# A list scheduler's price table and the place of one group of sums in a two-block kernel on one core

## Chip, cores and metric

The kernel runs on one core of one Trainium2 chip. The metric is the device time of one execution in microseconds (us), the median of several runs. In the profile PE is TensorE (matmuls), PEld its weight loads, DVE is VectorE, ACT is ScalarE, POOL is GpSimd and SP issues DMAs.

## The reference, cut to what matters

Two blocks of two layers each run one after the other on 512 tokens of width 1024 in fp32. The second block, around which the change lies, also carries 256 context tokens:

```
def hybrid_layer(l, x, xc, ...):                      # twice, l = 0 and 1
    h  = rms_norm(x,  norm_g) * (1 + scale)   + shift      # 512 tokens
    hc = rms_norm(xc, norm_g) * (1 + scale_c) + shift_c    # 256 tokens
    aq, ak, av, az, bq, ..., cq, ck, cv, cz, gm = split(h @ w_in)
    y_a = differential attention,  4 heads
    y_b = bidirectional mLSTM,     4 heads
    y_c = neighbourhood attention, 8 heads, done two at a time
    g   = sigmoid(gm)                                      # 3 x 1024 columns
    x   = x + gate * (sum_n g_n * (y_n @ w_br[n])) @ w_out
```

Before it, the first block has a recurrent mixer, a convolutional feed-forward layer, a forgetting attention with a spatial gate, and a second feed-forward layer. The reference computes in fp32 throughout.

## The kernel before

**Precision.** A weight matmul is done as three fp32r matmuls: each operand x is split into hi (an ACT copy to fp32r) and lo (a DVE subtraction x - hi), and `mm3` adds hi*hi, hi*lo and lo*hi in PSUM. `K.H` and `K.L` hold the hi and lo halves of the normed activations, eight tiles of 128 rows by 768 columns (512 tokens, then 256 of context). `modulated` writes them at the start of each layer of the second block: per row tile one DVE multiplication, one ACT copy to H and one DVE subtraction to L.

**The gate product.** The projection `gm` (3072 output columns) is done by a Strassen-Winograd scheme with 7 products in place of 8. It needs sums of quarters of the operand, made once per layer by `halves(n)`, a generator of four steps. One step takes two row tiles: two POOL additions H + L into tiles x and y, four DVE additions or subtractions of halves of x and y, and two splits (ACT copy, DVE subtraction) into four tiles that stay alive until the last gate product. In layer 0 (n = 384) all 768 columns take part, in layer 1 (n = 256) 512 columns. `gm_pair` makes two of 24 output tiles: it loads two weight tiles, makes their sums on POOL, and runs the seven products.

**Order of work.** `Block2.run` makes for each layer a list of 12 heads: 4 of branch C (two attention heads each), 4 of A, 4 of B. A head has a `prep` generator (projections of q, k, v; the splits and copies that stack them for PE, in `Kern.stack`) and an `attend` or `scan` generator (scores, softmax, products). At index i the loop weaves the second generator of head i with the `prep` of head i + 1, with `GM[i]` gate pairs (none before i = 3), and, in the kernel before, with `halves` at i = 0.

**The scheduler.** Nothing is issued in that order at once. `Order` records every instruction with its reads, writes and an estimated duration (`_cost`); `flush` then runs a list schedule. It keeps one clock for each engine; on each engine it scans up to 30 instructions whose producers have been placed, in the order of recording, takes the first that can start on time or else the one that starts first, and places the earliest of all engines. It adds a lag after each producer (190 to 250 ns between engines). The estimates thus set the fixed order of each engine's queue; they set no waits. The scheduler knows nothing of engines that slow one another.

**Slots.** All working tiles of the second block come from 36 slots called "s". An instruction may take a new tile only when at most `WINDOW` = 30 tiles of this kind recorded before it are still waiting for a slot, and only when its own tiles and up to 8 earlier ones would find free slots.

All instructions are recorded through a helper, so most rows of the profile carry its line, L486.

Of the kernel before, what the change touches and what calls it, by code (L numbers as in the profile page):

```python
# [199 lines left out]
class Order:  # L200
# [133 lines left out]
    @staticmethod  # L334
    def _cost(eng, op, a, k, aps, psum):
        size = 1
        n_in = 0
        for key, x in aps:
            n = 1
            for _, c in list(x.ap)[1:]:  # L340
                n *= c
            size = max(size, n)
            if key not in ("out", "accum_out", 0, "bias") and n > 4:
                n_in += 1
        if op == "dma_start":
            x = k["out"]
            b = 4
            for _, c in x.ap:
                b *= c
            return ("dma", b / 300.0)  # L350
        if eng == "pe":
            x = k["out"] if "out" in k else a[0]
            n = 1
            for _, c in list(x.ap)[1:]:
                n *= c
            if op == "transpose":
                return max(n, 64) / 1.2 + 3
            if k["rhs"].dtype == F32R:
                return n / 2.4 * (1 if n >= 256 else 2) + 3
            return max(n, 128) / 0.6 * (1 if x.ap[0][1] > 64 else 0.62) + 4  # L360
        if eng == "act":
            return (52 if psum else 94) + size * 0.833 + (93 if k.get("accum_out") is not None else 0)
        if eng == "pool":
            return 146 + (2.1 if op == "tensor_tensor" else 3.3) * size
        if op == "reciprocal":
            return 70 + 6.5 * size
        two = not psum and n_in <= 1 and op in ("tensor_copy", "tensor_scalar", "memset")
        return 95 + size / (1.92 if two else 0.96)


    def flush(self, keep=()):
# [120 lines left out]
def weave(*gens):  # L492

    live = [[0.5 / n, 1.0 / n, g] for n, g in gens]
    while live:
        x = min(live, key=lambda x: x[0])
        x[0] += x[1]
        if next(x[2], live) is live:
            live.remove(x)


def chain(*gens):

    def run():
        for _, g in gens:
            yield from g
    return sum(n for n, _ in gens), run()
# [656 lines left out]
FIRST = 7  # L1164

GM = (0, 0, 0, 1, 1, 1, 1, 2, 2, 2, 1, 1)


class Block2:
# [742 lines left out]
    def run(self, out, dbg, es):  # L1912
        K, nc = self.K, self.nc
        self.pool = es.enter_context(self.tc.tile_pool(name="slots", bufs=1))
        lat, ctx = K.part(0, T), K.part(T, TC)
        for l in range(2):
            self.l = l
            full = l == 0
            ya, yb, yc = [], [], []
            if l == 1:  # L1920
                for u in EARLY:
                    self.early[(1, *u)] = self.unit(*u, lat, ctx)
            hb, first = self.branch_b(lat, ctx, full, yb)
            heads = self.branch_c(lat, ctx, full, yc) + self.branch_a(lat, ctx, full, ya) + hb
            mg = []
            self.yd = {b: K.dr.tile([128, 4, 768], F32, name=f"yd{l}{b}") for b in (0, 2)}
            self.gd = [K.dr.tile([128, 8, 768], F32, name=f"gd{l}{b}") for b in range(3)]
            gm = [self.gm_pair(b, m) for b in (2, 0, 1) for m in range(0, 8, 2)]
            n = 384 if full else 256
            weave(heads[0][0])  # L1930
            for i in range(12):
                g = [gm.pop(0) for _ in range(GM[i])]
                weave(heads[i][1], *([heads[i + 1][0]] if i < 11 else []), *([first] if i == FIRST else []),
                      *([(4, self.halves(n))] if i == 0 else []),
                      *([chain(*((8, x) for x in g))] if g else []))
            for b, y in ((2, yc), (0, ya), (1, yb)):
                self.merge(b, y, mg, full, b == 1)
            X, S = self.out_proj(full, None if full or dbg == 6 else out)
            if dbg == 5 + l:
                for m in range(8):  # L1940
                    nc.sync.dma_start(out=out[:, m], in_=X[m])
                return
            if full:
                R, _ = S[0].rstd()
                for m in range(8):
                    nc.sync.dma_start(out=self.xd[:, m], in_=X[m])
                self.norm_lat(1, X, R, self.s)
# [36 lines left out]
```

## Time and profile before

| | us |
|---|---|
| median of 3 runs | 2893.25 |
| lowest, highest | 2891.59, 2897.68 |
| profiled execution, own time | 2893.14 |
| its span, first to last instruction | 2891.3 |
| PE busy (modelled) | 2832.5 |
| DVE, ACT, POOL busy | 2057.0, 1308.7, 402.3 |
| mean granted TensorE clock | 0.993 of full |

The span leaves 1.8 us of the execution's own time outside. Matmuls overlap in the pipeline and their ends are modelled, so PE's busy time is an upper bound of its work.

### The profile page before, as it was taken

The numbers are of one execution on the slowest core, as the hardware profiler recorded it, in microseconds if no ns is written. First come the engines' busy times: TensorE is split into PE (matmuls) and PEld (weight loads), VectorE is DVE, ScalarE is ACT, GpSimd is POOL, SyncE is SP. The second block draws the span as 40 slices with busy tenths as digits, with TensorE's granted clock in tenths as the row PEclk, the third lists the DMA queues.
The fourth block names the chain that finished last, engine by engine and source line by source line (L and its number), as shares of the span: only waits on it lengthen the run. The fifth ranks groups of instructions, "written<-read, shape, count | busy, mean of one in ns | idle before, by whom it ended". The sixth has DMA issues, their size and how long they took to land. (4 is left out here: it accounts for less than half of the span.)

```text
span 2891.3 us, 42552 instructions
## 1 busy us (share of the span) xinstructions
PE 2832.5 (98%) x16266; PEld 2444.7 (85%) x16266; DVE 2057.0 (71%) x4038; ACT 1308.7 (45%) x2469; POOL 402.3 (14%) x296
## 2 busy tenths in 40 slices
PE   8999999999999999999999999999999999999998
PEld 6888888887888888789999989998878889989887
DVE  7778678468786875865677686575686677787765
ACT  6344234455442343664455453341346554554433
POOL 1010000010100002200211132120220122232202
PEclk9999999999999999999999999999999999999999
DMA  4333433322333423211122132155322122233362
GB/s 157 125 119 123 136 139 111 105 96 96 124 111 129 144 87 124 79 61 63 56 77 75 55 108 92 68 162 173 124 74 93 63 76 75 78 100 103 103 211 95
DMA packets 113243, 302.63 MB, mean 105 GB/s; under 512 B 11656, under 2 KB 25352, under 8 KB 113040
## 3 DMA queue, kind: packets, MB, share of 16 engines
q1 hardware_dynamic: 112896, 299.91, 30.6%
q8 instruction: 128, 2.10, 0.3%
q14 instruction: 75, 0.61, 0.1%
q10 hardware_dynamic: 144, 0.00, 0.0%
HBM read 272.26 MB, written 27.61 MB: 104 GB/s over the span
## 5 line engine op out<-in xcount | busy, mean ns | idle before, releaser
L486 PE MATMUL P<-H,wl 128*128 128x512 f32 (+2 forms) x2648 | 962.2, 364 | 8.2 <-DVE wl L486 8.2
L486 PE MATMUL P<-H,wh 128*128 128x512 f32 (+2 forms) x2648 | 963.9, 365 | 2.7 <-ACT H L486 2.6
L486 PE MATMUL P<-L,wh 128*128 128x512 f32 (+2 forms) x2648 | 962.4, 364 | 3.4 <-DVE L L486 3.4
L486 ACT ACTIVATE wh<-ws 128x1024 fp32r<-128x1024 f32 (+3 forms) x450 | 436.4, 972 | 765.0 <-PE P L486 660.3
L486 DVE TENSOR_TENSOR wl<-ws,wh 128x1024 fp32r<-128x1024 f32 (+3 forms) x450 | 522.1, 1162 | 208.2 <-ACT wh L486 203.1
L486 PEld LDWEIGHTS P<-H,wl 128*128 128x128 f32 x2648 | 500.7, 189 | 88.0 <-DVE wl L486 10.5
L486 PEld LDWEIGHTS P<-L,wh 128*128 128x128 f32 x2648 | 500.5, 189 | 85.3 <-DVE L L486 6.5
L486 PEld LDWEIGHTS P<-H,wh 128*128 128x128 f32 x2648 | 500.6, 189 | 83.8 <-ACT H L486 3.7
L486 PE MATMUL P<-s,wh 128*128 128x256 f32 (+2 forms) x1344 | 329.7, 333 | 0.0
L486 PE MATMUL P<-t,wh 128*128 128x512 f32 x960 | 302.1, 395 | 0.7 <-ACT t L486 0.7
L486 ACT ACTIVATE s<-P 128x512 f32<-128x512 f32 (+3 forms) x436 | 189.9, 471 | 225.4 <-PE P L486 202.2
L486 PE MATMUL P<-s,s 128*128 128x128 f32 (+4 forms) x1616 | 246.6, 292 | 12.8 <-DVE s L486 12.7
L486 PEld LDWEIGHTS P<-s,wh 128*128 128x128 f32 x1344 | 228.9, 188 | 17.3
L486 PEld LDWEIGHTS P<-s,s 128*128 128x128 f32 (+1 forms) x1616 | 215.3, 190 | 32.8 <-issue 9.7
L486 PE MATMUL P<-s,wl 128*128 128x256 f32 (+2 forms) x672 | 222.3, 331 | 2.2 <-DVE wl L486 2.2
L486 PEld LDWEIGHTS P<-t,wh 128*128 128x128 f32 x960 | 179.9, 188 | 44.3 <-ACT t L486 0.9
L486 ACT ACTIVATE s<-s 128x768 f32<-128x768 f32 (+7 forms) x226 | 153.0, 694 | 110.2 <-DVE s L486 94.3
L486 POOL TENSOR_TENSOR s<-s,s 128x512 f32<-128x512 f32 (+2 forms) x87 | 112.4, 1299 | 583.3 <-DVE s L486 307.3
L486 DVE TENSOR_TENSOR s<-s,s 128x512 f32<-128x512 f32 (+8 forms) x205 | 179.3, 881 | 19.6 <-DMA s<-cmd 10.5
L486 PE MATMUL P<-t,wl 128*128 128x512 f32 x480 | 189.6, 395 | 0.0
L486 ACT ACTIVATE s<-P,tn 128x512 f32<-128x512 f32 (+1 forms) x226 | 119.0, 535 | 106.2 <-DVE tn L486 104.7
L486 ACT ACTIVATE t<-t 128x512 f32<-128x512 f32 (+4 forms) x162 | 97.8, 611 | 125.1 <-DVE t L486 124.2
(149 smaller groups left out, 3571.7 us busy)
## 6 DMA issues: line engine op xcount, KB each, us to landing
ws<-in_w2in SPq DMA_DIRECT2D x136, 512.0 KB, 3.3
ws<-in_up SPq DMA_DIRECT2D x88, 512.0 KB, 3.2
wm<-in_w_mod SPq DMA_DIRECT2D x48, 512.0 KB, 4.4
ws<-in_down SPq DMA_DIRECT2D x32, 384.0 KB, 3.1
ws<-in_w2br SPq DMA_DIRECT2D x48, 256.0 KB, 2.8
ws<-in_down SPq DMA_DIRECT2D x32, 320.0 KB, 2.8
ws<-in_w0in SPq DMA_DIRECT2D x18, 512.0 KB, 3.3
gd<-s SPq DMA_DIRECT2D x24, 384.0 KB, 2.9
```

The costliest lines, as they stand in the source:

```text
L486: o["f"](*o["a"], **o["k"])
```

## The change

Two edits. The first sets five prices of `_cost` anew: an fp32r matmul of n columns from n/2.4 + 3 ns to 0.4536 n + 1 ns; an ACT instruction whose scale or bias is a tile gets 91 ns more; a POOL tensor_tensor goes from 2.1 to 2.3 ns per element; a DVE copy, tensor_scalar or memset with at most one large input and nothing in PSUM goes from 95 to 130 ns of fixed part, every other DVE instruction (reciprocal apart) from 95 to 68 ns. The second weaves `halves` in at index 1, beside the second head and the prep of the third, and no longer at index 0.

```
             if k["rhs"].dtype == F32R:
-                return n / 2.4 * (1 if n >= 256 else 2) + 3
+                return n * 0.4536 * (1 if n >= 256 else 2) + 1
             return max(n, 128) / 0.6 * (1 if x.ap[0][1] > 64 else 0.62) + 4
         if eng == "act":
-            return (52 if psum else 94) + size * 0.833 + (93 if k.get("accum_out") is not None else 0)
+            per = any(hasattr(k.get(x), "tensor") for x in ("scale", "bias"))
+            return (52 if psum else 94) + size * 0.833 + (93 if k.get("accum_out") is not None else 0) + (91 if per else 0)
         if eng == "pool":
-            return 146 + (2.1 if op == "tensor_tensor" else 3.3) * size
+            return 146 + (2.3 if op == "tensor_tensor" else 3.3) * size
...
-        return 95 + size / (1.92 if two else 0.96)
+        return (130 if two else 68) + size / (1.92 if two else 0.96)
...
+HALF = 1
...
-                      *([(4, self.halves(n))] if i == 0 else []),
+                      *([(4, self.halves(n))] if i == HALF else []),
```

No instruction is added, removed or resized.

## Rows read from the trace of the kernel before

**Rows 1.** The page's busy time, share of the span and instructions of each engine.
```profile
PE 2832.5 (98%) x16266; PEld 2444.7 (85%) x16266; DVE 2057.0 (71%) x4038; ACT 1308.7 (45%) x2469; POOL 402.3 (14%) x296
```

**Rows 2.** Stretches of 50 us: busy us of each engine (instructions), PEclk, DMA, GB/s.
```profile
core 0: us, PE busy (x) PEld busy (x) DVE busy (x) ACT busy (x) POOL busy (x), PEclk, DMA share, GB/s
...
300.00:350.00 50.00, 50.00 (x216) 40.24 (x215) 34.72 (x62) 13.62 (x18) 0.00 (x0) 1.00 0.41 129
...
1150.00:1200.00 50.00, 43.78 (x267) 37.24 (x266) 42.97 (x83) 33.00 (x71) 18.06 (x8) 0.93 0.19 64
1200.00:1250.00 50.00, 50.00 (x369) 43.65 (x369) 35.74 (x91) 32.99 (x82) 0.00 (x0) 1.00 0.22 77
...
1700.00:1750.00 50.00, 45.78 (x268) 42.09 (x267) 35.96 (x73) 23.95 (x49) 18.97 (x12) 0.97 0.21 69
...
1800.00:1850.00 50.00, 50.00 (x345) 47.43 (x344) 24.30 (x50) 20.58 (x43) 13.06 (x11) 1.00 0.21 75
...
2200.00:2250.00 50.00, 49.76 (x350) 42.78 (x349) 28.50 (x81) 30.76 (x75) 2.29 (x2) 1.00 0.19 64
...
2350.00:2400.00 50.00, 48.82 (x305) 42.68 (x305) 45.09 (x94) 27.77 (x69) 13.20 (x9) 1.00 0.23 80
```

**Rows 3.** Waits of PE over the span: releaser, us in total, times, longest.
```profile
PE P L486 <- DVE s L486: 20.1, 20, 4.0
PE P L486 <- DVE wl L486: 11.0, 8, 2.6
PE P L486 <- DVE t L486: 4.8, 3, 3.0
```

**Rows 4.** Timeline of POOL in layer 0: start us, us, instruction, [idle before <- releaser].
```profile
1154.90 18.06 POOL L486 TENSOR_TENSOR s<-H,L 128x768 f32<-128x768 f32 x8 [34.08 <-DVE L L486]
...
1289.00 1.41 POOL L486 TENSOR_TENSOR ws<-ws,ws 128x512 f32<-128x512 f32 x1 [116.04 <-DVE wl L486]
```

**Rows 5.** Timeline of PE in layer 0, from 1163 to 1181 us.
```profile
1171.16 0.28 PE L486 MATMUL P<-H,wl 128*128 128x256 f32 x1
1175.49 0.55 PE L486 MATMUL P<-s,s 128*128 128x256 f32 x1 [4.05 <-DVE s L486]
```

**Rows 6.** Timeline of DVE in layer 0, from 1153 to 1181 us.
```profile
1157.12 5.33 DVE L486 TENSOR_TENSOR wl<-ws,wh 128x1024 fp32r<-128x1024 f32 x2 [2.44 <-ACT wh L486]
1164.12 2.93 DVE L486 TENSOR_TENSOR wl<-ws,wh 128x1024 fp32r<-128x1024 f32 x1 [1.67 <-ACT wh L486]
1166.96 2.20 DVE L486 TENSOR_TENSOR s<-s 128x384 f32<-128x384 f32 x1
1169.27 5.49 DVE L486 TENSOR_TENSOR s<-s,s 128x384 f32<-128x384 f32 x3
1174.79 1.02 DVE L486 CAST s<-s 64x768 fp32r<-64x768 f32 x2
```

**Rows 7.** Timeline of DVE after POOL has stopped, layer 0 and layer 1.
```profile
1183.32 0.95 DVE L486 TENSOR_TENSOR s<-s,s 128x768 fp32r<-128x768 f32 x1
1184.18 0.55 DVE L486 TENSOR_TENSOR s<-s 128x384 f32<-128x384 f32 x1
...
2148.80 1.22 DVE L486 TENSOR_TENSOR wl<-ws,wh 128x1024 fp32r<-128x1024 f32 x1
```

**Rows 8.** Timeline of ACT in layer 0, from 1163 to 1181 us.
```profile
1167.75 3.30 ACT L486 ACTIVATE s<-s 64x768 fp32r<-64x768 f32 x4
```

**Rows 9.** Stretches of 7 us at the heads of the two layers, columns as in Rows 2.
```profile
1171.00:1178.00 7.00, 2.95 (x16) 2.78 (x16) 6.81 (x8) 2.62 (x5) 1.96 (x1) 0.69 0.00 0
1178.00:1185.00 7.00, 7.00 (x44) 6.71 (x44) 5.31 (x17) 4.79 (x12) 0.00 (x0) 0.82 0.00 0
...
2160.00:2167.00 7.00, 4.01 (x20) 3.87 (x20) 5.82 (x15) 4.26 (x10) 0.00 (x0) 0.76 0.21 78
```

**Rows 10.** Timeline of PE in layer 1: its three waits.
```profile
2133.60 0.50 PE L486 MATMUL P<-L,wh 128*128 128x512 f32 x1 [0.70 <-DVE L L486]
2142.34 0.50 PE L486 MATMUL P<-L,wh 128*128 128x512 f32 x1 [1.48 <-DVE L L486]
...
2163.07 3.11 PE L486 MATMUL P<-s,s 128*128 128x256 f32 x15 [2.99 <-DVE s L486]
```

**Rows 11.** Timeline of DVE in layer 1, from 2131 to 2166 us.
```profile
2133.47 2.05 DVE L486 SCALAR_TENSOR_TENSOR s<-s,gs,P 128x512 f32<-128x512 f32 x3
...
2138.75 1.46 DVE L486 TENSOR_TENSOR s<-s 128x256 f32<-128x256 f32 x1
2140.31 1.32 DVE L486 TENSOR_TENSOR s<-s,s 128x256 f32<-128x256 f32 x1
...
2157.64 0.42 DVE L486 TENSOR_TENSOR s<-s 128x256 f32<-128x256 f32 x1
```

## The prediction

> **What bounds the kernel now.** Read the page first: PE is busy for 2832.5 of 2891.3 us [rows 1], so 58.8 us of idle PE is the first thing to look for. Then the stretches: where PE is full, as in the feed-forward layers, 216 matmuls of 512 columns fill 50 us [rows 2], 231.5 ns each. No queue order changes that rate, and no instruction is added or removed, so the change can only move PE's idle time and its clock. The waits of PE say what ends its idle time: DVE, with the three largest groups together 35.9 us [rows 3]. The stretches say where: 1150 to 1200 us has 6.22 us of idle PE and a mean granted clock of 0.93 [rows 2]. That is the head of layer 0 of the second block, where `halves` runs. The last view is the timeline there, engine by engine. The reader is to see one POOL block of 18.06 us [rows 4], DVE instructions under it that take twice their usual time [rows 6, 7], and PE at the end of its work waiting 4.05 us for DVE [rows 5].
>
> **The moved sums: what leaves the head of layer 0.** POOL's eight additions run from 1154.90 to 1172.96. DVE's instructions in that time: two weight splits in 5.33 us, one in 2.93, a sum in 2.20, then a sum and two stacking subtractions (three) in 5.49 [rows 6]. Free of POOL they take 1.22, 0.55 and 0.95 us [rows 7]. Extra: 5.33 - 2.44 = 2.89; 2.93 - 1.22 = 1.71; 2.20 - 0.55 = 1.65; 5.49 - (0.55 + 0.95 + 0.95) = 3.04; together 9.3 us. Two sums also stand ahead of the stacking of the first head, on which the first score matmul waits. PE runs dry at about 1171.28 (a start at 1171.16 and half of 231.5 ns for 256 columns) and starts again at 1175.49 [rows 5].
>
> With `halves` gone, what is late next? The ACT splits of the stack end at 1171.05, those of the first attention head half-way through, at 1169.4 [rows 8]. Then one DVE subtraction (0.95) and two casts (1.02) [rows 6, 7] give 1171.4 us, plus some 0.2 of signalling (an estimate). The wait shrinks from 4.05 to about 0.4 us: 3.65 gained. After that wait the granted clock is at its lower level, 1.2 of 2.4 GHz, for (1 - 0.69) x 7 / 0.5 + (1 - 0.82) x 7 / 0.5 = 6.9 us [rows 9]; half of it, 3.4 us, is lost work. Without the wait there is no fall. Layer 0: 7.0 us, bounds 0 and 7.5.
>
> **What leaves the head of layer 1.** Here the sums run among the instructions that still write L. PE waits 0.70 and 1.48 us for L, and 2.99 us for the stack [rows 10]. Before the second wait stand two sums of 1.46 and 1.32 us [rows 11], 0.42 each when free [rows 11]: without them L comes 2.8 us earlier, more than the wait. Before the third stand most of the other 14 sums and eight splits; by 0.42 and about 0.63 (two thirds of the 0.95 of layer 0 [rows 7], an estimate) that is 11 us of DVE, more than the 5.2 us of all three waits. The clock after it is low for (1 - 0.76) x 7 / 0.5 = 3.4 us, 1.7 lost [rows 9]. Layer 1: 0.70 + 1.48 + 2.99 + 1.7 = 6.9 us, bounds 0 and 6.9.
>
> **What the sums cost beside the second head.** Sixteen POOL additions, 32 DVE sums and 16 splits move; no DMA is among them, so SP's queue stays. They land about where the stretches 1200 to 1250 and 2200 to 2250 lie, with PE at 50.00 and 49.76, POOL at 0.00 and 2.29 us [rows 2]. In layer 0 DVE then has its 35.74 us, 16 x 0.55 + 8 x 0.95 = 16.4 us of sums and splits, and the same 9.3 us of slowing if POOL runs in one block: 61 us, more than one stretch holds, so they spread into the next. Behind the slowed instructions on DVE stand the score maxima, the softmax scalings and the weight splits, and for all three PE waits. Nothing shows this mix directly; the nearest rows are stretches with as much POOL work. With 18.97 us of it PE idles 4.22 us and the clock (0.97) loses another 1.5; with 13.20 it idles 1.18; with 13.06, 0.00 [rows 2]. So layer 0 pays 0 to 5.7, layer 1 (18.06 x 2/3 = 12.0 us of POOL) 0 to 1.2. I take 2.2 and 0.8, below the middle in layer 0, since the projections of the third head are there as filling work and nothing is due: the first gate pair comes at i = 3. Together 3.0.
>
> The rule that speaks against the change: the Trainium skill, SBUF — State Buffer, section Who interferes with whom, says that a DVE instruction with two SBUF inputs and a GpSimd instruction that reads SBUF exclude each other, the later one standing still until the other is done. The 5.33 us for two splits agree [rows 6]. By it the eight additions lock DVE out just as long beside the second head, and if every such microsecond came back as PE idle, the cost would be 9.3 + 6.2 in place of my 3.0.
>
> **The prices.** The new PE price for 512 columns is 233.2 ns, the old 216.3, the trace 231.5: the error goes from -7% to +1%. The DVE price of an instruction with two operands of 512 falls from 628 to 601 ns, while three such took 2.05 us, 683 each [rows 11]: that one moves away. ACT and POOL move up. All this re-deals the queue orders of 2893 us. Where PE is full it costs nothing, since every order keeps it full. What is at stake are the waits outside the two heads: 35.9 - 4.05 - 2.99 = 28.9 us [rows 3, 5, 10]. They could all go, or as many come. There is a reason for a loss: with PE priced too fast, the scheduler put more filling work than needed between a DVE chain and the matmul that uses it; 24 matmuls of filling hid 24 x 15.2 ns = 0.36 us of delay that it does not know of, such as POOL's. I take 1.5 us lost, 6 either way (a fifth of 28.9, an estimate).
>
> **Sum.** 2893.14 - 7.0 - 6.9 + 3.0 + 1.5 = 2883.7 us against the profiled execution's own time; that execution lies 0.1 us under the median of 2893.25, so 2884 beside the median.
>
> **The rivals.**
> *The stall moves along.* POOL's block goes to the second head and PE waits there as long as it did before. (The rule above would give this.) For it: DVE fills more than the stretch. Against it: from 1800 to 1850 PE never stood still under 13.06 us of POOL [rows 2]. Time: 2893.1 + 1.5 = about 2894.6.
> *The margin goes* (slower). Place: the softmax chains, 80 in the second block (8 heads by 6 tiles, 8 by 4) and 16 in the forgetting attention. Each loses up to 0.36 us of hiding; at 96 x 0.36 = 35 us in all. It decides, that is the kernel becomes more than 0.2% slower, once it costs 10.9 + 5.8 = 16.7 us, 46 chains of 96. Against it: PE waits for DVE `s` only 20 times now [rows 3], so most chains have more room. At 60 chains: 2882.2 + 21.6 = about 2904.
> *The sums do not move.* POOL takes what is ready, whatever its place in the program, and its next work comes only at 1289.00 [rows 4]. Against it: in layer 0 the first sum tile stands behind 13 + 27 + 13 = 53 tiles (a prep, an attend, a prep of branch C, counted in the code), in layer 1 behind 45, and only 30 may be waiting. Time: 2893.1 + 1.5 = 2894.6, or less if they come late but still in the first head.
>
> **How the numbers follow.** A change that a measurement of this kernel can tell from none is about 0.2%, 5.8 us; the runs shown spread by that. My forecast, chance 0.60: 2884, its own range 2876 to 2889. The stall moves along, 0.18: 2890 to 2898. The sums do not move, 0.10: the same. The margin goes, 0.12: from 2895 up. The range to hold 8 in 10 runs from 2875 to 2896: it leaves out most of the margin's case and a little of each tail. Faster by over 0.2% needs under 2887.5: nearly all of the forecast and a little of the sums that come later in the first head, 0.61. Within 0.2%: most of the two middle cases, 0.24. Slower: 0.15, from the margin and the worst of the moved stall.
>
> **What would show it.** Right: POOL's additions of H and L start after 1190 us; the wait of 4.05 us is under 1 and PEclk between 1150 and 1200 us is 1.00; between 2100 and 2200 us the three waits are gone; the feed-forward stretches still hold 216 matmuls in 50 us. The cost: DVE instructions of 2 us or more, and PE waits of up to 2 us, between 1200 and 1260 us. Wrong: a new fall of the clock within the second head, POOL's block where it was, or waits of PE for `s` well above 20 in number outside the heads.

## The result, and the profile after

| | before | after |
|---|---|---|
| median, us | 2895.47 (4 runs) | 2920.94 (4 runs) |
| lowest, highest | 2891.59, 2898.73 | 2920.71, 2923.13 |
| ratio, 95% interval | | 1.0093 [1.0078, 1.0108] |
| span of the profiled execution | 2891.3 | 2919.2 |
| mean granted clock | 0.993 | 0.991 |

The change made the kernel 0.93% slower by this ratio (25.5 us between the two medians), where 0.3% faster was forecast. The page after, busy time of each engine, answers to [rows 1]:

```profile
PE 2843.1 (97%) x16266; PEld 2448.7 (84%) x16266; DVE 2061.0 (71%) x4038; ACT 1319.0 (45%) x2469; POOL 407.5 (14%) x296
```

The instructions are the same in number. The span grew by 27.9 us and PE's busy time by 10.6: PE stands still for 76.1 us in place of 58.8, and part of what counts as busy is work at the lower clock. The waits of PE after (releaser, us in total, times, longest) answer to [rows 3]:

```profile
PE P L487 <- DVE s L487: 38.4, 31, 3.2
PE P L487 <- DVE wl L487: 7.7, 6, 3.4
PE P L487 <- ACT s L487: 7.3, 7, 3.2
PE P L487 <- DVE t L487: 5.0, 5, 1.9
```

Weight splits (`wl`) cost less than before, tiles `s` written by DVE 18.3 us more. The stretches after, columns as in [rows 2]:

```profile
300.00:350.00 50.00, 50.00 (x216) 40.39 (x215) 32.26 (x57) 13.04 (x18) 0.00 (x0) 1.00 0.42 134
1150.00:1200.00 50.00, 42.70 (x279) 35.41 (x279) 33.50 (x74) 33.01 (x70) 11.29 (x6) 0.97 0.22 75
1200.00:1250.00 50.00, 46.78 (x316) 40.19 (x315) 39.79 (x95) 31.80 (x79) 6.50 (x2) 0.97 0.19 62
...
2350.00:2400.00 50.00, 46.71 (x301) 41.92 (x300) 41.63 (x84) 26.94 (x64) 11.96 (x8) 0.97 0.25 77
```

The feed-forward stretch holds its 216 matmuls. The stretch from 1200 us, full before with 369 matmuls, now has 316 and 3.22 us of idle PE. Where the rest arises is seen by counting matmuls from the start and comparing when PE begins the n-th (the orders differ, so this is good to some us): the 5600th begins 2.6 us earlier than before (at 1206 us), the 8400th 13.7 us later (at 1620), the 12000th 12.7 later (at 2217), the 14800th 29.9 later (at 2629), the 16000th 27.7 later. The loss thus has two places, the attention and mLSTM heads of layer 0 and those of layer 1, and it begins behind the stretch for which the gain was forecast.

One such wait, in the timeline of PE (start us, us, instruction, [idle before <- releaser]):

```profile
1226.98 0.29 PE L487 MATMUL P<-H,wl 128*128 128x256 f32 x1
1227.10 0.28 PE L487 MATMUL P<-H,wh 128*128 128x256 f32 x1
1230.60 1.94 PE L487 MATMUL P<-C,s 128*128 128x128 f32 x8 [3.22 <-ACT s L487]
```

`P<-C,s` are transposes of softmax tiles. What they wait for is a chain that crosses between DVE and ACT (score mask, maximum, exponential, sum, scaling). The timeline of DVE in the same place:

```profile
1226.76 0.41 DVE L487 CUSTOM_DVE_ANT_0 s<-P,s 128x256 f32<-128x256 f32 x1
1227.10 0.08 DVE L487 DVE_READ_ACCUMULATOR2_ANT tn<- 128x1 f32 x1
1227.10 1.22 DVE L487 TENSOR_TENSOR wl<-ws,wh 128x1024 fp32r<-128x1024 f32 x1
1228.24 0.20 DVE L487 TENSOR_SCALAR tn<-tn 128x1 f32<-128x1 f32 x1
1229.57 0.16 DVE L487 TENSOR_TENSOR tn<-tn 128x2 f32<-128x2 f32 x1 [1.12 <-ACT s L487]
...
1229.96 0.88 DVE L487 TENSOR_SCALAR s<-s,tn 128x512 f32<-128x512 f32 x2
```

At 1227.10 a weight split of 1.22 us gets ahead of a 0.20 us link of the chain; then DVE waits 1.12 us for ACT's exponentials, and the scaling that the transposes read begins at 1229.96. ACT in the same place:

```profile
1228.48 0.47 ACT L487 ACTIVATE s<-P,tn 128x256 f32<-128x256 f32 x1 [0.55 <-DVE tn L487]
...
1229.44 1.08 ACT L487 ACTIVATE s<-P 128x512 f32<-128x512 f32 x1
```

PE had been out of other work since about 1227.2: its queue puts the transposes next. The trace names ACT as releaser: its copy out of PSUM, queued behind these exponentials, ends at 1230.52, just before the transposes start at 1230.60. Of the delay about 0.55 us is the split's, the time for which ACT stands idle for the late link; the rest is the length of the chain itself. More matmuls queued between the scores and the transposes would have covered it, and there were plenty: the projections merely stand behind the transposes.

### The profile page after: what moved, and what is told of

Its sections match the earlier page's. It is cut to its first block, busy times and chain, and to the rows that moved or that the text cites. A ratio compares the mean times of both kernels' runs of the same rounds, so it can differ in the third digit from the quotient of the medians.

```text
span 2919.2 us, 42561 instructions
## 1 busy us (share of the span) xinstructions
PE 2843.1 (97%) x16266; PEld 2448.7 (84%) x16266; DVE 2061.0 (71%) x4038; ACT 1319.0 (45%) x2469; POOL 407.5 (14%) x296
## 5 line engine op out<-in xcount | busy, mean ns | idle before, releaser
L487 ACT ACTIVATE s<-s 128x512 f32<-128x512 f32 (+7 forms) x226 | 153.2, 694 | 123.7 <-DVE s L487 97.7
L487 DVE TENSOR_TENSOR s<-s,s 128x512 f32<-128x512 f32 (+7 forms) x205 | 178.3, 876 | 25.1 <-ACT s L487 14.2
```

The costliest lines, as they stand in the source:

```text
L487: o["f"](*o["a"], **o["k"])
```

## The experiments

The theory to begin with: the new price of PE's matmuls makes the scheduler queue the transposes too early, since its prices of the softmax chains are too short (the rival called "The margin goes"). Against it stood: the moved sums cost the time; the other prices do. Each edit is shown against the kernel that its paragraph names, the kernel before or the change; all ratios are against the kernel before, run again beside each set of kernels (medians 2892.12 to 2892.59 us), with the 95% interval.

**The parts, one at a time.** The prices without the moved sums, that is the change with the sums back beside the first head:

```
-HALF = 1
+HALF = 0
```

> The new prices with the sums left beside the first head. Theory A (the prices take the filling work out from under the softmax chains): most of the 25 us loss is here, ratio 1.005 to 1.010, and the time that PE needs from an fp32r matmul to a following transpose stays near the 64 us of the changed kernel (40 us before). Theory B (the sums beside the second head slow the chains there): ratio 0.998 to 1.002.

The moved sums without the prices:

```
-                      *([(4, self.halves(n))] if i == 0 else []),
+                      *([(4, self.halves(n))] if i == 1 else []),
```

> The old prices with the sums beside the second head. Theory A: no loss, and a gain if the prediction's first part held (ratio 0.995 to 1.001). Theory B: ratio 1.005 to 1.010. Under both, PE's wait of 4.05 us at the head of layer 0 should be gone if the sums leave DVE's queue ahead of the stack.

The change with only PE's price put back:

```
-                return n * 0.4536 * (1 if n >= 256 else 2) + 1
+                return n / 2.4 * (1 if n >= 256 else 2) + 3
```

> The changed kernel with the old price of an fp32r matmul alone (n/2.4 + 3). Theory A1 (it is PE's own price, 7% too low before, that gave the chains their filling work): nearly all of the loss comes back, ratio 0.996 to 1.002. Theory A2 (it is the lower fixed part of DVE, 68 for 95 ns, or the ACT part): ratio stays at 1.005 to 1.010. Theory B: ratio stays at 1.005 to 1.010.

The kernel before with only PE's price new:

```
-                return n / 2.4 * (1 if n >= 256 else 2) + 3
+                return n * 0.4536 * (1 if n >= 256 else 2) + 1
```

> The kernel before with the new price of an fp32r matmul alone (0.4536 n + 1). Theory A1: ratio 1.004 to 1.010, with more and longer waits of transposes for the softmax. Theory A2 and theory B: 0.998 to 1.002.

| kernel | median, us | ratio |
|---|---|---|
| prices only | 2920.12 | 1.0097 [1.0082, 1.0112] |
| sums only | 2895.18 | 1.0010 [1.0001, 1.0020] |
| change, old PE price | 2897.72 | 1.0017 [1.0007, 1.0026] |
| before, new PE price | 2923.24 | 1.0106 [1.0091, 1.0121] |

One line, PE's price, is the whole loss, with either place of the sums. The four other prices together make no difference beyond the intervals here (1.0017 beside 1.0010). The sums, for which 10.9 us of gain had been worked out, give none.

**PE's price in steps.** If it is the direction of the error that counts, a price even further from the measured duration must be faster than the kernel before.

```
-                return n / 2.4 * (1 if n >= 256 else 2) + 3
+                return n / 2.6 * (1 if n >= 256 else 2) + 3
```

> The kernel before with the fp32r price lowered further, n/2.6 + 3 (199.9 ns for 512 columns, 14% under the trace). Theory A1 (filling work hides what the scheduler does not know of the softmax chains): the 17 us that transposes still wait in the kernel before shrink, ratio 0.993 to 0.999. Rival C (any change of a price re-deals the queues and the kernel before merely drew well): no order in the price, ratio 1.002 to 1.010.

`n / 2.9` in the same line:

> The kernel before with n/2.9 + 3 (179.6 ns for 512 columns, 22% under the trace). Theory A1: as good as n/2.6 or some us worse, since the filling work of a head runs out before its last chains; ratio 0.992 to 1.003, with waits of transposes under 17 us. Rival C: anything from 1.000 to 1.012.

`n * 0.435 ... + 2`, about halfway to the new price:

> The kernel before with the fp32r price half-way to the new one (0.435 n + 2, 224.7 ns for 512 columns). Theory A1: about half of the loss of the new price alone, ratio 1.003 to 1.008. Rival C: no order, either under 1.002 or over 1.009.

The new PE price, with longer lags on the chain's two engines:

```
-    LAG = {"pe": 190, "act": 230, "dve": 250, "pool": 250, "sp": 100}
+    LAG = {"pe": 190, "act": 290, "dve": 310, "pool": 250, "sp": 100}
```

> The new fp32r price alone, but the lags after ACT and DVE raised by 60 ns each (290 and 310). A softmax chain has some six such hand-overs, so the scheduler puts about 0.36 us more of filling work into each, what the dearer matmul had taken out. Theory A1: the loss of 1.0106 comes back, ratio 0.995 to 1.002. Rival C: the loss stays within half of its size, 1.005 or more.

The ratios are 0.9970 [0.9958, 0.9983] for n/2.6, 0.9939 [0.9924, 0.9954] for n/2.9, 1.0063 [1.0048, 1.0078] for the middle price and 1.0072 [1.0057, 1.0087] for the lags. The time follows PE's price in order, through the old price and out beyond it: the worse the price fits the matmul, the faster the kernel, down to 2874.53 us, which beats both. Longer lags gave back only a third of the loss, where nearly all had been expected: this one forecast missed, and rival C's was met. The scheduler's own reckoning, below, says how little the lags did. The waits of PE for `s` from DVE in three of these kernels, new price on the kernel before, n/2.6, n/2.9:

```profile
PE P L486 <- DVE s L486: 32.7, 39, 3.9
```

```profile
PE P L486 <- DVE s L486: 18.7, 22, 3.6
```

```profile
PE P L486 <- DVE s L486: 15.9, 16, 3.4
```

**The other side of the ratio.** If only the relation of PE's price to the chain's counts, PE's measured price must do no harm once the chain is priced longer too. All prices of ACT and DVE and their lags times 1.12, PE's price new (new lines only):

```
+    LAG = {"pe": 190, "act": 258, "dve": 280, "pool": 250, "sp": 100}
...
+                return n * 0.4536 * (1 if n >= 256 else 2) + 1
...
+            return 1.12 * ((52 if psum else 94) + size * 0.833 + (93 if k.get("accum_out") is not None else 0))
...
+            return 1.12 * (70 + 6.5 * size)
...
+        return 1.12 * (95 + size / (1.92 if two else 0.96))
```

> The new fp32r price, and every price of ACT and DVE and their lags 12% up on those of before. Theory A1 in its sharper form (what counts is the ratio of PE's price to that of the softmax chains; the chains really last about a tenth longer than the scheduler thinks, so a true PE price alone makes it put the transposes too early): as good as the kernel before or a little better, ratio 0.995 to 1.003. Rival D (a dearer PE as such makes the queues worse, whatever the others cost): 1.006 to 1.012.

0.9986 [0.9977, 0.9995], 2888.74 us: the loss of 1.06% is gone, with PE's price at its measured value, so a dear PE as such does no harm (rival D fell). What counts is PE's price beside those of ACT and DVE. The edit lengthens these everywhere, not in the softmax chains alone, so this run doesn't separate the chains from other work of the two engines; the next part looks at the chains themselves.

**What the scheduler believes, and what happens.** The recorded program has one order on each engine, so each instruction can be put beside its record in the trace. There are 152 groups of softmax transposes, one for each softmax tile of the forgetting attention and of branches A and C. For them, four numbers: entries of PE's queue between the last score matmul that the group's chain needs and its first transpose; the room between the end of the chain's last instruction, a DVE scaling, and the first transpose's start; how many groups have under 0.25 us of room; and the time that PE lost between a matmul of the projections and a transpose right behind it (starts' distance less 231.5 ns for 512 columns, fewer in proportion, summed over all transposes, the few of values and head outputs included). The first two are medians.

| kernel | ratio | entries between | room, us | under 0.25 us | lost, us |
|---|---|---|---|---|---|
| n/2.9 | 0.9939 | 55.5 | 1.27 | 9 | 4.1 |
| n/2.6 | 0.9970 | 49 | 0.87 | 13 | 12.9 |
| new PE price, chain x 1.12 | 0.9986 | 46 | 0.82 | 28 | 10.2 |
| before (n/2.4) | 1 | 41 | 0.50 | 45 | 17.0 |
| middle price | 1.0063 | 40 | 0.38 | 59 | 25.6 |
| new PE price, longer lags | 1.0072 | 39 | 0.30 | 71 | 28.9 |
| new PE price | 1.0106 | 38 | 0.22 | 88 | 29.5 |
| the change, old PE price | 1.0017 | 42 | 0.63 | 33 | 27.4 |
| the change | 1.0093 | 36 | 0.26 | 72 | 40.4 |

The first seven kernels differ only in prices and lags and have the sums in the same place; their median room falls in the same order as their time grows. From the start of the last score matmul to the end of the chain, the scheduler of the kernel before reckons 6.21 us and the chip takes 6.82 (medians), 10% more. With PE's price new it reckons 5.96 and the chip takes 6.57; longer lags raise the reckoning only to 6.19, less than the 0.36 us that had been expected of them. With the chain's prices times 1.12 it reckons 7.48 and the chip takes 7.06. So the kernel before had two errors, PE 7% too fast and the chain about 10% too short, and they largely cancelled; the change mended one.

The lost time is only part of the loss. With PE's price alone new it grew by 12.5 us, about half of the 26.4 us by which the profiled span grew; time at the lower clock rose from 40.3 to 51.8 us, which is some 6 us of slower work, in part the same time; waits for tiles `s` written by POOL rose from 2.1 to 8.2 us. For the change it grew by 23.4 of 27.9 us, but the change with the old PE price, 1.0017, already loses 27.4, and what it gains back elsewhere was not traced.

**How far it goes, and whether the rest of the change matters then.** n/3.4, and n/2.9 on the change and with the moved sums:

```
-                return n / 2.4 * (1 if n >= 256 else 2) + 3
+                return n / 3.4 * (1 if n >= 256 else 2) + 3
```

> The kernel before with the fp32r price n/3.4 + 3 (153.6 ns for 512 columns, a third under the trace). Theory A1 has a lower end: once the transposes no longer wait, a lower price can give nothing more and spends the filling work of a head too early. Flat against n/2.9 or a little worse, ratio 0.993 to 0.998. If the gain goes on at the rate of the four points so far (some 0.3% per 20 ns), 0.988 to 0.991, and something else than those waits is being paid back.

The change with `n / 2.9` in that line:

> The changed kernel with the fp32r price alone set to n/2.9 + 3, so that the new prices of ACT, POOL and DVE and the moved sums stay. If PE's price relative to the chains is the whole cause, it lands within 0.2% of the kernel with n/2.9 and nothing else changed: ratio 0.992 to 0.996. If the other prices or the sums have a harm of their own that the PE price hid, 0.997 or more.

The kernel before with `n / 2.9` and the sums at `i == 1`:

> The fp32r price n/2.9 + 3, everything else as before, and the sums beside the second head. Theory E (the sums' place is worth nothing either way: the stall at the head of layer 0 goes and comes back in the second head): within 0.15% of the same price with the sums beside the first head, ratio 0.992 to 0.996. Theory F (with room in the chains the moved sums cost nothing there, and the gain of some 10 us that was forecast appears): 0.989 to 0.992.

n/3.4 gives 1.0154 [1.0138, 1.0169], 2937.24 us: worse than any price tried, which neither theory had expected. The transposes are well covered (median room 1.61 us), but the weight splits are not, so the order by room ends here. Its waits of PE:

```profile
PE P L486 <- DVE wl L486: 32.0, 16, 6.3
PE P L486 <- DVE s L486: 13.7, 16, 2.2
```

The first was 11.0 us before [rows 3]. Time at the lower clock is 79.6 us in place of 40.3, so about 20 of the 42.7 us by which this span is longer are slower work. The change with n/2.9 gives 0.9956 [0.9942, 0.9971], from 1.0093 by that one line; the kernel before with n/2.9 and the moved sums gives 0.9935 [0.9920, 0.9950], the same as 0.9939 with the sums in their old place. The other four prices, without effect above, cost 0.2% here (0.9956 beside 0.9935), at the edge of the intervals.

**What the sums cost, and where.** The sums moved but not gained: is it POOL that slows DVE in either place? The additions H + L on POOL become ACT copies of H, so that POOL has nothing to do there (L is left out of these sums, and ACT has eight more instructions in each layer):

```
-                nc.gpsimd.tensor_tensor(a, K.H[:, r, :2 * n].bitcast(F32), K.L[:, r, :2 * n].bitcast(F32), op=ALU.add)
+                nc.scalar.activation(a, K.H[:, r, :2 * n].bitcast(F32), AF.Copy)
```

> The kernel before with the sums beside the first head, but H + L is replaced by an ACT copy of H, so that POOL does nothing there; the part L of the gate product's operand is left out. Theory G (POOL's additions slow DVE down and so make the 4.05 us wait and the fall of the clock): the weight splits at the head take 1.2 us each, the wait shrinks to under 1 us, ratio 0.995 to 0.999. Rival H (DVE's own sums ahead of the stack make it): the wait stays above 2 us, ratio 0.999 to 1.001.

The same with the sums at `i == 1`:

> The same without POOL (the part L of that operand left out), with the sums beside the second head, old prices. Theory G: the loss of 3 to 5 us between 1206 and 1321 us that the moved sums brought is gone, ratio 0.994 to 0.998. Rival H: the sums' DVE work costs it, ratio 1.000 to 1.002 as with POOL.

And the sums, POOL's additions included, beside the third head (`i == 2`):

> Old prices, the sums woven in beside the third head, one further than in the change. Theory E (POOL starts on the sums when it finds free slots, whatever their place in the program, so a place two heads on shifts only part of them): ratio 0.999 to 1.002 again. Theory F' (one head on was too near; two heads on the sums leave the heads of both layers and the forecast gain of some 10 us appears): 0.995 to 0.998.

Without POOL: 0.9983 [0.9973, 0.9992] beside the first head, 0.9967 [0.9954, 0.9979] beside the second. Against the same place with POOL, POOL's additions are worth 0.17% (4.9 us) beside the first head and 1.0010 - 0.9967 = 0.43% (12.4 us) beside the second. Beside the third head, with POOL, 0.9983 [0.9974, 0.9993]: a gain of 4.9 us, a little under half of the 10.9 worked out for the second; where it arises was not traced. The two kernels without POOL differ in more than POOL: the copies read H alone, so these sums no longer wait for L, and ACT has more to do. What POOL's additions are worth is therefore shown together with that wait.

The timeline of POOL with only the sums moved (`i == 1`), which answers to [rows 4]:

```profile
1154.22 3.66 POOL L486 TENSOR_TENSOR s<-H,L 128x768 f32<-128x768 f32 x2 [34.08 <-DVE L L486]
1183.83 4.99 POOL L486 TENSOR_TENSOR s<-H,L 128x768 f32<-128x768 f32 x2 [25.94 <-ACT s L486]
1192.90 5.74 POOL L486 TENSOR_TENSOR s<-H,L 128x768 f32<-128x768 f32 x2 [4.09 <-DVE s L486]
1206.12 6.05 POOL L486 TENSOR_TENSOR s<-H,L 128x768 f32<-128x768 f32 x2 [7.48 <-PE P L488]
```

DVE of the same kernel under the second of these, and just after:

```profile
1183.70 0.95 DVE L486 TENSOR_TENSOR s<-s,s 64x768 fp32r<-64x768 f32 x1
...
1184.84 2.31 DVE L486 TENSOR_TENSOR s<-s,s 64x768 fp32r<-64x768 f32 x1
1187.19 2.30 DVE L486 TENSOR_SCALAR s<-s,tn 128x512 f32<-128x512 f32 x2
...
1190.61 0.88 DVE L486 TENSOR_SCALAR s<-s,tn 128x512 f32<-128x512 f32 x2
```

And its PE in the same place:

```profile
1178.19 0.50 PE L486 MATMUL P<-H,wh 128*128 128x512 f32 x1 [1.55 <-ACT s L486]
...
1189.24 0.66 PE L486 MATMUL P<-C,s 128*128 128x128 f32 x2 [2.27 <-DVE s L486]
```

The wait of 4.05 us for the stack [rows 5] is gone, as forecast. In its place comes 1.55 us for ACT a little later. What ACT does there:

```profile
1176.28 1.28 ACT L486 ACT_TABLE_LOAD   x1
1177.58 0.47 ACT L486 ACTIVATE s<-P,tn 128x256 f32<-128x256 f32 x1
```

The first exponential, which reads a score tile out of PSUM, stands behind a table load of 1.28 us; PE goes on as soon as it is done. The prediction's account of what is late next has no table load. And the block of POOL, no longer in one piece, falls on softmax chains: a subtraction takes 2.31 us in place of 0.95, two scalings 2.30 in place of 0.88, and the transposes behind them wait 2.27 us. Both slowed kinds agree with the Trainium skill, SBUF — State Buffer, section Who interferes with whom: a DVE instruction with two SBUF inputs contends with a GpSimd one that reads SBUF, and a tensor_scalar in one of DVE's two-port modes contends with GpSimd too. In which mode these scalings ran no run shows. The first pair of additions does not move at all (1154.22, before 1154.90): the new place puts them later in the list, yet the scheduler finds their inputs and slots free.

At equal matmul counts the kernel with the sums alone moved is 1.6 us ahead at 1206 us, about 0.5 us behind from 1261 to 1291 us, 3.4 us behind at 1304 and 1321 us, gains 2.9 in layer 1, and ends 1.5 us behind. So it loses 2.1 us beside the second head. The next 2.9 us, between 1291 and 1304 us, are not the sums' work on DVE: PE has the same two waits there in the kernel before and with the sums moved.

```profile
1293.47 0.63 PE L486 MATMUL P<-C,s 128*128 128x128 f32 x4 [1.77 <-DVE s L486]
1294.87 0.52 PE L486 MATMUL P<-C,s 128*128 128x128 f32 x3 [0.78 <-ACT s L486]
```

```profile
1294.02 0.63 PE L486 MATMUL P<-C,s 128*128 128x128 f32 x4 [1.77 <-DVE s L486]
1295.42 0.87 PE L486 MATMUL P<-C,s 128*128 128x128 f32 x3 [0.78 <-ACT s L486]
```

The first two are of the kernel before, whose granted clock stays at 1.00 from 1294 to 1301 us; with the sums moved it is 0.57 there. These are single executions, so a difference of this kind may belong to the execution and not to the kernel; that the sums gain nothing overall rests on the medians.

## Why the prediction was wrong

**The step that failed: the prices, "1.5 us lost, 6 either way".** That term measured +28 to +31 us (1.0097 for all prices, 1.0106 for PE's alone). The mechanism was in the text, as the rival "The margin goes", at the right place and in the right direction, with a ceiling of 35 us, and was given 0.12 on one row: that PE waits for `s` only 20 times [rows 3]. That row tells how many chains are late, not how near the others are. In the kernel before 45 of 152 groups had under 0.25 us of room, half had under 0.50, and the rival's own 0.36 us for each chain was over two thirds of that. Room was to be had from the trace of before: the distance between the end of a DVE scaling and the start of its transposes. What the rival lacked was why the room was so small: it took the 7% on PE as spare, but it was paying for chains about 10% too short.

**The head of layer 0, -7.0 us.** The step "The wait shrinks from 4.05 to about 0.4 us" holds for that one wait. What is late next was named one link too early: behind the scores comes a wait of 1.55 us for ACT's first exponential behind its table load, and it is there with POOL's work moved or taken out beside the second head (1.55 and 1.54 us). POOL's first pair stayed. "Without the wait there is no fall" holds from 1171 to 1185 us, where the granted clock is 1.00 in place of 0.69 and 0.82 [rows 9]; but it falls at 1189 us, where PE has just waited 2.27 us for the softmax, so the stretch 1150 to 1200 us has 0.97 with the sums moved, and about half of the 3.4 us is lost again. Measured by 1206 us: -1.6 us, of which 0.7 were there at 1135 us, before the head begins.

**The head of layer 1, -6.9 us.** With only the sums moved, the wait of 2.99 us is gone, the waits for L are 0.71 and 0.73 in place of 0.70 and 1.48 [rows 10]. Measured: -2.9 us with the cost beside the second head in it, against -6.9 + 0.8.

**The sums beside the second head, +3.0 us.** In layer 0 measured 2.1 us beside the second head, where 2.2 was forecast; with the 2.9 us of lower clock at 1294 us it is 5.0, inside the bounds of 0 to 5.7. The reason given, that nothing is due there, was wrong: the softmax chains of the first two heads are due there, and the size came out right without it. Nor is this trace the whole cost: without POOL's additions, and without their wait for L, the kernel with the sums beside the second head was 12.4 us faster over both layers, nearer to the 9.3 + 6.2 = 15.5 us that the prediction named as the other way than to its 3.0. The three terms together, -10.9 us, came out as +0.10% (+2.9 us by the ratio).

**Right.** The feed-forward stretches did not change; the block of POOL split up, and under it DVE's instructions were slow in the new place too (2.31 us for 0.95); "the sums do not move" fell for all but the first pair. "The stall moves along" comes nearest to what the sums by themselves did, but its time, 2894.6 beside the measured 2895.18 us, agrees by luck: it holds 1.5 us for the prices, which this kernel has not got. The signs named for a wrong prediction, a fall of the clock (0.97 between 1200 and 1250 us) and more waits for `s`, both came.

**What stays open.** That the ratio of prices is the cause is shown by the runs; through which waits all of the loss comes is not, since the transposes hold about half of it. Why n/3.4 loses at the weight splits is not shown, only that it does. Which prices between n/2.9 and n/3.4 are best was not tried, nor whether prices of the chain measured link by link would reach the 0.9939 of n/2.9.

## What to carry to other kernels

A list scheduler's prices act as ratios: when one engine's price is corrected, measure the chains on the others against the scheduler's own clock in the same edit, or a balance of two errors breaks. Before trusting a small number of waits, look at the room of those that do not wait; here the median was 0.50 us. And moving work in the recording order moves it in time only if something then holds it back, and to a better place only if what runs there is not due.

## What the runs showed of the hardware

Between 1200 and 1250 us the granted clock was 1.00 before [rows 2] and 0.97 after; the only idle time of PE in it is the wait of 3.22 us, and the clock is at its lower level right behind it (0.57 on average from 1230 to 1234 us). The same waits don't always go with the same clock: the pair of 1.77 and 0.78 us above had 1.00 in one kernel and 0.57 in the other. Time under the lower clock over the span rose from 40.3 to 52.6 us, so about 6 of the 27.9 us are slower work. A weight split of 128x1024 that takes 2.93 us under POOL [rows 6] takes 1.22 with POOL's additions gone at the same place, the timeline of DVE without them beside the first head:

```profile
1163.62 1.22 DVE L486 TENSOR_TENSOR wl<-ws,wh 128x1024 fp32r<-128x1024 f32 x1 [4.14 <-ACT wh L486]
```

PE still stood still in that kernel, now for ACT, whose copies in place of POOL's additions stand ahead of the table load and the first exponential:

```profile
1181.76 0.79 PE L486 MATMUL P<-H,wh 128*128 128x512 f32 x1 [4.91 <-ACT s L486]
```

So theory G's forecast for the time came true there and its forecast for the wait, under 1 us, did not. A head wait of nearly 5 us and a faster kernel go together, as do the 3.36 us at the same head with n/2.9: the one long wait that is easiest to see doesn't decide the time.
